# Stick-breaking attention on one core: low parts of the keys in one tile per head, doubled over the partitions, and a second score product over 128 rows instead of 64

## The chip, the core and the metric

The kernel runs on one core of one Trainium2 chip, as one launch. A core has a matrix engine (PE in the profile, TensorE in words), a vector engine (DVE, VectorE), an engine for activation functions (ACT, ScalarE), a general engine (POOL, GpSimd) and a queue that issues the transfers here (SP, SyncE). PE works in two instructions per product: a weight load (`LDWEIGHTS`, the rows PEld) of the operand that stays in the array, and the `MATMUL` that streams the other operand past it into a PSUM bank. The metric is the device time of the program in microseconds (us): 1305.93 us, the median of 3 runs before the change (1305.73 to 1306.77).

## The reference

A decoder trunk of two layers over 1024 tokens of width 1024, batch 1. Layer A is a gated short convolution. Layer B is attention with 16 heads of width 64, in which the weight of a key is a sigmoid times the product of (1 - sigmoid) over all keys between it and the query. The part that matters here, cut:

```python
def stick_breaking_attention(q, k, v):
    ...
        z = jnp.einsum('bhqd,bhkd->bhqk', qb, kb) * inv_sqrt_d
        ...
        mask = kpos < qpos
        log_beta = jax.nn.log_sigmoid(z)
        log_1m_beta = jnp.where(mask, log_beta - z, 0.0)
        suffix = lax.cumsum(log_1m_beta, axis=3, reverse=True) - log_1m_beta
        a = jnp.where(mask, jnp.exp(log_beta + suffix), 0.0)
        outs.append(jnp.einsum('bhqk,bhkd->bhqd', a.astype(vb.dtype), vb))
```

Around it stand the projections of q, k, v and a gate from the normed input, an output projection, a residual and a last norm. All of it is float32.

## The kernel before, in words

**Precision.** PE multiplies float32 data of a shortened form (`F32R`). To keep the precision, an operand x is split into a high part h (rounded to the short form) and a low part l = x - h, and a product of two operands is summed from h·h, h·l and l·h. A projection (`linear`, lines 176 to 178) is therefore three `MATMUL`s per 128 input channels, 24 per 512 tokens.

**Keys and queries.** Heads come in pairs, 8 pairs; a pair's 128 channels lie on the 128 partitions, head A (a = 0) on partitions 0 to 63 and head B (a = 1) on 64 to 127. After the projection, `keys` writes with `evacuate` (line 443 on ACT, line 444 on DVE) the high parts of both heads into one tile and the low parts into the tile `kl`. Three transfers per half of the tokens (`move`, line 440, issued by SP, 64 partitions x 512 tokens, 128 KB) then build two tiles `kh[0]`, `kh[1]`, each with the high part of one head's keys in both halves of the partitions. `queries` builds `qq[0]`, `qq[1]` likewise: the high part of one head's queries in that head's half, its low part in the other half. All these tiles are of 128 x 1024 numbers and come from the pool tag `qk`, which has 10 buffers; a pair takes five (`kl`, two `kh`, two `qq`).

**Scores.** `attention` goes, for each head a of the pair, over four groups g of two blocks of 128 queries and over chunks of up to 512 keys. Per block and chunk there are two products into one PSUM bank (tag `z`, 2 banks), with the query block of `qq` as the weights:

- line 524: all 128 rows, `qq[:, qs]` with `kh`, which gives high queries · high keys plus low queries · high keys in one pass;
- line 525: the 64 rows `own` of the head, `qq[own, qs]` with `kl[own, ...]`, which adds high queries · low keys.

A head has 12 such pairs of products: 6 that are 512 keys wide and 2 each of 384, 256 and 128; a pair of heads has 24, the program 192. Behind them follows, per block: two sigmoids on ACT (lines 530, 531), a scan on DVE (line 535), a product on POOL (line 537), transposes on PE (line 546), the split of the transposed block on ACT and DVE (lines 549, 550), and the products with the values on PE (lines 559, 560); the head's output is put together on ACT and DVE (lines 564, 565).

**Order.** The main loop runs over the pairs: attention of pair p, then the gate's projection `silu_z(p)` and the projections `project_qkv(p + 1)` of the next pair; weights are prepared by a transfer (line 144), a scaling on DVE (line 151), a split on ACT and POOL (lines 138, 139) and a sum over the shift on DVE (lines 159, 161). In the program as built the instructions of each engine stand in an order that a scheduler fixed beforehand, so that the projections of the next pair fill PE's time between the steps of the running pair's attention. Each engine works its own list from front to back and waits on semaphores of the others. SP's queue is such a list too: a transfer that waits holds up those behind it. In the last pair the place of the next projections is taken by the first part of the output projection.

Of the kernel before, what the change touches and what calls it, by code (L numbers as in the profile page):

```python
# [15 lines left out]
P = 128          # partitions  # L16
D = 1024         # model width
T = 1024         # tokens
KT = D // P      # contraction tiles
HALF = 512       # tokens per PSUM bank  # L20
NH = T // HALF
DH = 64          # head width
NPAIR = 8        # pairs of heads
EPS = 1e-6
SPILL = NPAIR - 2  # pairs whose gated output waits in DRAM
EARLY = 4        # output tiles begun before the last pair is done
WARM = (6, 6, 3)  # idle products behind the first loads
# [4 lines left out]
# columns of the packed vectors  # L32
# [4 lines left out]
def decoder_kernel(ctx, tc, vecs, xT, a_mod, kv_mod, b_mod, w_in, w_out_a, w_kv, w_qz, w_out_b, outT):  # L37
# [20 lines left out]
    # ---- constants  # L58
    vec = const.tile([P, 128], F32, name="vec")
    nc.sync.dma_start(vec, vecs)  # L60
    # zeros, then the identity: what the scan over a row of blocks adds on the diagonal
# [17 lines left out]
    # ---- [128, n * 128] -> the sums over the partitions, n columns of 128, as groups of up to 4  # L79
# [14 lines left out]
    # ---- the same as products that add up in PSUM: a sum over sources, each with its column of factors  # L94
    def column_totals(terms, n):
        ps = ps_tile("o")[:, :n]
        for k, (src, factor) in enumerate(terms):
            for i in range(n):
                # one start for the bank: the first write to each column after it replaces, the others add
                nc.tensor.matmul(ps[:, i:i + 1], lhsT=src[:, i * P:(i + 1) * P], rhs=factor,  # L100
                                 start=(k == 0 and i == 0), stop=(k == len(terms) - 1 and i == n - 1))
        return ps

    # ---- the modulation's vectors, one number per partition and column
# [15 lines left out]
    # products that nobody reads, so that TensorE's clock is up when the first ones are due  # L120
# [20 lines left out]
    # ---- weights: gain folded in, split in two parts of 12 bits, and the shift's share  # L141
# [38 lines left out]
    # ---- sums of squares by channel -> 1/rms by token, the same in every partition  # L180
# [38 lines left out]
    # ======== layer A: gated short convolution ========  # L219
# [12 lines left out]
    # the gain of one half of the channels, two row tiles of the modulation's weights at a step  # L232
# [138 lines left out]
    # ---- out-projection of layer A, residual, sums of squares  # L371
# [27 lines left out]
    # ======== layer B: stick-breaking attention ========  # L399
# [27 lines left out]
    def normalise(sl):  # L427
        # from here on these tokens have their rms in the input of layer B's projections
        for kt in range(KT):
            x = att.tile([P, HALF], F32, name="xn", tag="b", bufs=6)  # L430
            nc.sync.dma_start(x, x1_dram[kt, :, sl])
            nc.vector.tensor_mul(x, x, rbc_b[:, sl])
            split(x1h[kt][:, sl], x1l[kt][:, sl], x, nc.gpsimd)

    def project_qkv(p):
# [11 lines left out]
        # kh: the high part of one head's keys, twice; kl: the low parts of both heads' keys  # L447
        kl = qk_tile("kl")
        kh = [qk_tile("kh") for _ in range(2)]

        def keys(sl, t, bias):
            evacuate(t, bias, kh[0][:, sl], kl[:, sl])
            move(kh[1][A, sl], kh[0][B, sl])
            move(kh[1][B, sl], kh[0][B, sl])
            move(kh[0][B, sl], kh[0][A, sl])

        # qq: the high part of one head's queries, and its low part in the other half
# [11 lines left out]
        def values(src, bias):  # L469
            t = att.tile([P, HALF], F32, name="vt", tag="pt", bufs=2)  # L470
            nc.scalar.activation(t, src, AF.Identity, bias=bias)
            ps = ps_tile("tr")
            for i in range(4):
                nc.tensor.transpose(ps[:, i * P:(i + 1) * P], t[:, i * P:(i + 1) * P], ident)
            # columns: A hi, A lo, B lo, B hi
            v = att.tile([P, 4, 4, DH], F32R, name="vv", tag="vv", bufs=4)
            src = ps.rearrange("p (b a d) -> p b a d", b=4, a=2)
            nc.scalar.activation(v[:, :, 0::3, :], src, AF.Copy)
            nc.vector.tensor_tensor(v[:, :, 1:3, :], src, v[:, :, 0::3, :].bitcast(F32), op=ALU.subtract)
            vv.append(v)  # L480
# [19 lines left out]
        return [(kh[a], kl, qq[a]) for a in range(2)], vv  # L500
# [3 lines left out]
    def attention(p, heads, vv):  # L504
        o = att.tile([P, T], F32, name="o", tag="o", bufs=2)
        for a in range(2):
            kh, kl, qq = heads[a]
            own, oth = half(a), half(1 - a)
            for g in range(4):
# [5 lines left out]
                for c in reversed(range(g // 2 + 1)):  # L515
                    c0 = c * HALF
                    rows = []
                    for r in range(2):
# [6 lines left out]
                        nc.tensor.matmul(zps[:, :w], lhsT=qq[own, qs], rhs=kl[own, c0:c0 + w], start=False, stop=True)  # L525
                        b = att.tile([P, HALF], F32, name="b", tag="b", bufs=6)
                        # suffix products: a row of blocks ends in column T - 1, and column T holds zeros
# [4 lines left out]
                        # from the right: 0 above the diagonal, 1 on it, then the product of the columns passed  # L532
# [6 lines left out]
                    for jp in reversed(range(2 * c, min(2 * c + 2, g + 1))):  # L539
# [3 lines left out]
                        # blocks by (key block, query block); the last key block has one query block  # L543
# [55 lines left out]
    # ---- out-projection of layer B, residual, last norm  # L599
# [20 lines left out]
    # while the last pair's attention runs: the other pairs' share of the first tiles  # L620
# [116 lines left out]
```

## Time and profile before

| | |
|---|---|
| time, median of 3 runs | 1305.93 us (1305.73 to 1306.77) |
| profiled execution, from the first to the last instruction (span) | 1303.0 us |
| median less span (launch and end, outside the instructions) | 2.9 us |
| PE busy | 1223.5 us, 94% |
| DVE busy | 1066.1 us, 82% |
| POOL busy | 584.8 us, 45% |
| ACT busy | 507.1 us, 39% |
| transfers' share of the 16 DMA engines (main queue) | 30.3% |

The profile gives for the profiled execution the span alone, so its own whole time is taken as the span and the 2.9 us around it; a change in the span is carried over to the median of the runs. Busy times of PE are modelled: a `MATMUL` row lasts until its last result is written, while the next one starts earlier, so the time that a product takes of PE is the step from its start to the start of the next. Attention stretches from about 564 us to about 1195 us; what lies ahead is layer A and the modulation, what lies behind is the rest of the output projection and the last norm. In a row of the stretches (windows) the numbers behind an engine's name are busy us and, in brackets, instructions; PEclk is the granted clock of TensorE as a share of full speed.

### The profile page before, as it was taken

The numbers are of one execution on the slowest core, as the hardware profiler recorded it, in microseconds if no ns is written. First come the engines' busy times: TensorE is split into PE (matmuls) and PEld (weight loads), VectorE is DVE, ScalarE is ACT, GpSimd is POOL, SyncE is SP. The second block draws the span as 40 slices with busy tenths as digits, with TensorE's granted clock in tenths as the row PEclk, the third lists the DMA queues.
The fourth block names the chain that finished last, engine by engine and source line by source line (L and its number), as shares of the span: only waits on it lengthen the run. The fifth ranks groups of instructions, "written<-read, shape, count | busy, mean of one in ns | idle before, by whom it ended". The sixth has DMA issues, their size and how long they took to land.

```text
span 1303.0 us, 16390 instructions
## 1 busy us (share of the span) xinstructions
PE 1223.5 (94%) x5828; PEld 977.0 (75%) x5828; DVE 1066.1 (82%) x1575; ACT 507.1 (39%) x928; POOL 584.8 (45%) x393
## 2 busy tenths in 40 slices
PE   5899799879889999888999999999999999999995
PEld 4688588668777888766777777777777777777885
DVE  7989876888988746799889888899888898678366
ACT  3412221111211232235555555545555455556251
POOL 4623332323323354276455544646446465447334
PEclk9999899889998999888999999999999999999997
DMA  9332214243343444441212122121121212352203
GB/s 367 151 98 65 83 49 145 89 137 123 96 153 107 140 149 131 126 141 61 53 49 82 49 61 54 65 66 49 61 53 65 70 46 67 99 222 98 65 18 130
DMA packets 56450, 128.02 MB, mean 98 GB/s; under 512 B 6576, under 2 KB 10800, under 8 KB 56368
## 3 DMA queue, kind: packets, MB, share of 16 engines
q1 hardware_dynamic: 56368, 126.97, 30.3%
q8 instruction: 46, 0.75, 0.2%
q14 instruction: 36, 0.29, 0.1%
HBM read 99.68 MB, written 14.68 MB: 88 GB/s over the span
## 4 chain that ended last, share of the span: by engine, by line
PE 65%; DVE 25%; DMA 6%; issue 2%; ACT 0%; POOL 0%; SPq 0%; DVEq 0%; POOLq 0%; ACTq 0%
PE ps_mm L176 11%; PE ps_mm L177 11%; PE ps_mm L178 10%; DVE bacc L161 7%; PE ps_z L525 5%; PE ps_tr L546 5%; DVE gacc L116 4%; PE ps_o L560 3%; PE ps_o L559 3%; PE ps_z L524 3%; DMA graw<-b_mod 3%; PE ps_z L177 2%; PE ps_z L176 2%; PE ps_z L178 2%; DVE s L327 2%
## 5 line engine op out<-in xcount | busy, mean ns | idle before, releaser
L537 POOL TENSOR_TENSOR b<-b,sfx 128x128 f32<-128x128 f32 (+1 forms) x192 | 207.5, 1089 | 260.0 <-DVE sfx L535 195.8
L139 POOL TENSOR_TENSOR wlo<-raw,whi 128x1024 fp32r<-128x1024 f32 x78 | 197.5, 2534 | 281.8 <-ACT whi L138 255.4
L535 DVE TENSOR_TENSOR_SCAN sfx<-sfx,zid 128x128 f32<-128x128 f32 (+1 forms) x192 | 225.3, 1187 | 17.9 <-ACT sfx L530 17.7
L176 PE MATMUL ps_mm<-x1h,whi 128*128 128x512 f32 x480 | 195.7, 408 | 0.1
L177 PE MATMUL ps_mm<-x1l,whi 128*128 128x512 f32 x480 | 193.3, 403 | 0.0
L178 PE MATMUL ps_mm<-x1h,wlo 128*128 128x512 f32 x480 | 192.2, 400 | 0.0
L138 ACT ACTIVATE whi<-raw 128x1024 fp32r<-128x1024 f32 x78 | 82.5, 1058 | 172.0 <-issue 71.6
L530 ACT ACTIVATE sfx<-ps_z 128x128 f32<-128x128 f32 (+1 forms) x192 | 95.6, 498 | 88.4 <-PE ps_z L525 86.5
L549 ACT ACTIVATE ah<-ps_tr 128x512 fp32r<-128x512 f32 (+1 forms) x160 | 85.2, 560 | 79.2 <-PE ps_tr L546 77.1
L550 DVE TENSOR_TENSOR al<-ps_tr,ah 128x512 fp32r<-128x512 f32 (+1 forms) x160 | 96.5, 625 | 22.6 <-ACT ah L549 21.9
L161 DVE SCALAR_TENSOR_TENSOR bacc<-raw,shift_a,bacc 128x128 f32<-128x128 f32 x196 | 107.7, 561 | 2.8
L176 PEld LDWEIGHTS ps_mm<-x1h,whi 128*128 128x128 f32 x480 | 91.3, 190 | 23.7 <-issue 6.2
L177 PEld LDWEIGHTS ps_mm<-x1l,whi 128*128 128x128 f32 x480 | 91.1, 190 | 21.6 <-issue 5.4
L178 PEld LDWEIGHTS ps_mm<-x1h,wlo 128*128 128x128 f32 x480 | 91.0, 190 | 20.6 <-issue 3.3
L531 ACT ACTIVATE b<-ps_z 128x128 f32<-128x128 f32 (+1 forms) x192 | 96.1, 500 | 9.4 <-PE ps_tr L546 9.4
L116 DVE SCALAR_TENSOR_TENSOR gacc<-graw,cs,gacc 128x512 f32<-128x512 f32 x84 | 67.0, 802 | 39.0 <-DMA graw<-kv_mod 17.9
L546 PE MATMUL ps_tr<-zid,b 128*128 128x128 f32 x576 | 91.0, 275 | 1.2 <-POOL b L537 1.2
L559 PE MATMUL ps_o<-ah,vv 128*128 128x256 f32 x320 | 86.7, 288 | 0.0
L525 PE MATMUL ps_z<-kl,qq 64*128 64x128 f32 (+1 forms) x192 | 84.5, 440 | 0.0
L560 PE MATMUL ps_o<-al,vv 128*128 128x256 f32 x320 | 81.7, 294 | 0.5 <-DVE al L550 0.4
L161 DVE SCALAR_TENSOR_TENSOR bacc<-raw,shift_b,bacc 128x128 f32<-128x128 f32 x112 | 76.2, 680 | 1.3
L524 PE MATMUL ps_z<-kh,qq 128*128 128x128 f32 (+1 forms) x192 | 75.4, 393 | 0.0
(246 smaller groups left out, 2764.7 us busy)
## 6 DMA issues: line engine op xcount, KB each, us to landing
raw<-w_in SPq DMA_DIRECT2D x28, 512.0 KB, 4.2
graw<-b_mod SPq DMA_DIRECT2D x48, 256.0 KB, 2.7
stage<-a_mod SPq DMA_DIRECT2D x16, 512.0 KB, 9.6
graw<-kv_mod SPq DMA_DIRECT2D x32, 256.0 KB, 3.1
raw<-w_kv SPq DMA_DIRECT2D x16, 512.0 KB, 3.6
raw<-w_qz SPq DMA_DIRECT2D x16, 512.0 KB, 3.8
kh<-kh SPq DMA_DIRECT2D x48, 128.0 KB, 2.3
raw<-w_out_b SPq DMA_DIRECT2D x10, 512.0 KB, 3.7
```

The costliest lines, as they stand in the source:

```text
L116: nc.vector.scalar_tensor_tensor(acc[:, sl], raw, cs[:, kt:kt + 1], acc[:, sl], op0=ALU.mult, op1=ALU.add)
L139: lo_eng.tensor_tensor(lo, full, hi.bitcast(F32), op=ALU.subtract)
L161: nc.vector.scalar_tensor_tensor(acc, raw[:, kt * P:(kt + 1) * P], shift[:, kt:kt + 1], acc, op0=ALU.mult, op1=ALU.add)
L176: nc.tensor.matmul(ps, lhsT=wh, rhs=ah[kt][:, sl], start=(kt == kts[0]), stop=False)
L177: nc.tensor.matmul(ps, lhsT=wh, rhs=al[kt][:, sl], start=False, stop=False)
L178: nc.tensor.matmul(ps, lhsT=wl, rhs=ah[kt][:, sl], start=False, stop=(kt == kts[-1]))
L525: nc.tensor.matmul(zps[:, :w], lhsT=qq[own, qs], rhs=kl[own, c0:c0 + w], start=False, stop=True)
L535: nc.vector.tensor_tensor_scan(rev, rev, zid[:, z0:z0 + w][:, ::-1], sf[r][:, s0 + w:s0 + w + 1], op0=ALU.mult, op1=ALU.add)
L537: nc.gpsimd.tensor_tensor(b[:, :w], b[:, :w], sf[r][:, s0 + 1:s0 + w + 1], op=ALU.mult)
L546: nc.tensor.transpose(tp[:, s * P:(s + 1) * P], rows[r][:, jb * P - c0:(jb + 1) * P - c0], ident)
L559: nc.tensor.matmul(ops[:, cols], lhsT=vs, rhs=ah[:, rs], start=first, stop=False)
L560: nc.tensor.matmul(ops[:, cols], lhsT=vs, rhs=al[:, rs], start=False, stop=end)
```

## The change: what it does

`kl` becomes a list of two tiles. The evacuation writes the low parts of both heads into `kl[0]`, and the same three transfers that `kh` had build `kl[0]` and `kl[1]`, each with the low parts of one head's keys in both halves of the partitions. The second score product reads all 128 rows of `qq` and of the head's own `kl`; it adds high queries · low keys and also low queries · low keys. A pair takes six tiles of the tag `qk` instead of five; the tag keeps 10 buffers. Comments are removed, which moves some line numbers by one: lines 524 and 525 of before are 525 and 526 after, 474 is 475, 546 is 547.

```diff
-        # kh: the high part of one head's keys, twice; kl: the low parts of both heads' keys
-        kl = qk_tile("kl")
+
+        kl = [qk_tile("kl") for _ in range(2)]
         kh = [qk_tile("kh") for _ in range(2)]
 
         def keys(sl, t, bias):
-            evacuate(t, bias, kh[0][:, sl], kl[:, sl])
-            move(kh[1][A, sl], kh[0][B, sl])
-            move(kh[1][B, sl], kh[0][B, sl])
-            move(kh[0][B, sl], kh[0][A, sl])
+            evacuate(t, bias, kh[0][:, sl], kl[0][:, sl])
+            for k in (kh, kl):
+                move(k[1][A, sl], k[0][B, sl])
+                move(k[1][B, sl], k[0][B, sl])
+                move(k[0][B, sl], k[0][A, sl])
...
-        return [(kh[a], kl, qq[a]) for a in range(2)], vv
+        return [(kh[a], kl[a], qq[a]) for a in range(2)], vv
...
                         nc.tensor.matmul(zps[:, :w], lhsT=qq[:, qs], rhs=kh[:, c0:c0 + w], start=True, stop=False)
-                        nc.tensor.matmul(zps[:, :w], lhsT=qq[own, qs], rhs=kl[own, c0:c0 + w], start=False, stop=True)
+                        nc.tensor.matmul(zps[:, :w], lhsT=qq[:, qs], rhs=kl[:, c0:c0 + w], start=False, stop=True)
```

On SP's queue, in a middle pair, the transfers from one weight load to the next but one stand in the built program of before as:

```order
L144 DMA raw<-w_kv 128x1024
L440 DMA kh<-kh 64x512 x6
L144 DMA raw<-w_qz 128x1024
L440 DMA qq<-qq 64x512
L440 DMA qq<-ql 64x512 x2
L440 DMA qq<-qq 64x512
L440 DMA qq<-ql 64x512 x2
L144 DMA raw<-w_kv 128x1024
```

and in that of the change as:

```order
L144 DMA raw<-w_kv 128x1024
L440 DMA kh<-kh 64x512 x2
L440 DMA kl<-kl 64x512 x2
L440 DMA kh<-kh 64x512
L440 DMA kl<-kl 64x512
L440 DMA kh<-kh 64x512 x2
L440 DMA kl<-kl 64x512 x2
L440 DMA kh<-kh 64x512
L440 DMA kl<-kl 64x512
L144 DMA raw<-w_qz 128x1024
L440 DMA qq<-qq 64x512
```

Six transfers are added per pair, all ahead of the load of the query weights (`w_qz`); what follows keeps its order.

In the last pair, the load of one residual tile (line 611, the fifth of eight) also goes behind the twelve loads of the gated outputs (line 625).

On PE, DVE, ACT and POOL the lists of before and after hold the same arithmetic instructions, and apart from the first pair's attention they stand in the same order row by row. In the first pair some rows change places. On PE, around the transposes of the first pair's second half of values (`vt`), before:

```order
L176 MATMUL ps_mm<-x1h,whi 128x512
L524 MATMUL ps_z<-kh,qq 128x384
L525 MATMUL ps_z<-kl,qq 128x384
L177 MATMUL ps_mm<-x1l,whi 128x512
L178 MATMUL ps_mm<-x1h,wlo 128x512
L176 MATMUL ps_mm<-x1h,whi 128x512
L474 MATMUL ps_tr<-zid,vt 128x128 x4
L524 MATMUL ps_z<-kh,qq 128x512
L525 MATMUL ps_z<-kl,qq 128x512
```

and after:

```order
L176 MATMUL ps_mm<-x1h,whi 128x512
L475 MATMUL ps_tr<-zid,vt 128x128 x4
L177 MATMUL ps_mm<-x1l,whi 128x512
L178 MATMUL ps_mm<-x1h,wlo 128x512
L176 MATMUL ps_mm<-x1h,whi 128x512
L177 MATMUL ps_mm<-x1l,whi 128x512
L178 MATMUL ps_mm<-x1h,wlo 128x512
L525 MATMUL ps_z<-kh,qq 128x384
L526 MATMUL ps_z<-kl,qq 128x384
L525 MATMUL ps_z<-kh,qq 128x512
L526 MATMUL ps_z<-kl,qq 128x512
```

The score products of 384 and 512 keys stand a few projection products later, behind the transposes instead of around them. (The rows show the partitions of the output; the 64 rows of line 525 are its operands'.)

## The prediction

> **What bounds the kernel now.** I read the page first (span, busy shares, the chain of work that ended last), then the stretches pair by pair, then the timeline around a score product. From the page, its span, its busy times and the chain:
>
> ```profile
> span 1303.0 us, 16390 instructions
> PE 1223.5 (94%) x5828; PEld 977.0 (75%) x5828; DVE 1066.1 (82%) x1575; ACT 507.1 (39%) x928; POOL 584.8 (45%) x393
> ...
> PE ps_mm L176 11%; PE ps_mm L177 11%; PE ps_mm L178 10%; DVE bacc L161 7%; PE ps_z L525 5%; PE ps_tr L546 5%; DVE gacc L116 4%; PE ps_o L560 3%; PE ps_o L559 3%; PE ps_z L524 3%; DMA graw<-b_mod 3%; PE ps_z L177 2%; PE ps_z L176 2%; PE ps_z L178 2%; DVE s L327 2%
> ```
>
> Lines 524 and 525 stream equally many columns, yet the chain has 5% of the span for line 525 and 3% for line 524. The stretches (first pair in two parts, pairs 1 to 5, pair 6, the last pair's attention) say who sets the pace:
>
> ```profile
> 564.00:604.00 40.00, 31.26 (x116) 23.19 (x114) 39.75 (x55) 17.16 (x33) 28.11 (x19) 0.83 0.31 98
> 604.00:661.00 57.00, 57.00 (x283) 43.41 (x281) 48.70 (x69) 31.27 (x62) 31.18 (x23) 1.00 0.23 61
> 661.00:742.00 81.00, 80.98 (x408) 62.97 (x409) 72.33 (x96) 42.98 (x90) 38.96 (x33) 1.00 0.21 59
> 742.00:822.00 80.00, 80.00 (x405) 62.32 (x403) 70.48 (x96) 42.53 (x89) 38.34 (x32) 1.00 0.21 60
> 822.00:902.20 80.20, 80.20 (x405) 62.56 (x404) 71.36 (x97) 42.70 (x89) 41.95 (x33) 1.00 0.20 60
> 902.20:982.50 80.30, 80.30 (x406) 62.64 (x405) 71.17 (x97) 42.68 (x89) 41.95 (x33) 1.00 0.20 60
> 982.50:1062.80 80.30, 80.30 (x406) 62.64 (x405) 71.17 (x97) 42.69 (x89) 41.93 (x33) 1.00 0.20 60
> 1062.80:1144.50 81.70, 81.70 (x420) 64.07 (x418) 61.14 (x80) 43.13 (x90) 41.17 (x34) 1.00 0.28 88
> 1144.50:1192.50 48.00, 48.00 (x250) 36.54 (x248) 37.98 (x45) 30.46 (x66) 25.45 (x21) 1.00 0.49 176
> ```
>
> The columns are length, PE, PEld, DVE, ACT, POOL, granted clock, DMA share, GB/s. From 604 on PE is never idle, at full clock; a pair takes 80.3 us, and DVE is second with 71.2. Whether PE is busy with work is a question of the steps from one product's start to the next. The timeline:
>
> ```profile
> 811.35 0.40 PE L176 MATMUL ps_mm<-x1h,whi 128*128 128x512 f32 x1
> ...
> 811.58 0.39 PE L177 MATMUL ps_mm<-x1l,whi 128*128 128x512 f32 x1
> 811.58 0.19 PEld L178 LDWEIGHTS ps_mm<-x1h,wlo 128*128 128x128 f32 x1
> 811.81 0.39 PE L178 MATMUL ps_mm<-x1h,wlo 128*128 128x512 f32 x1
> ...
> 812.04 0.40 PE L524 MATMUL ps_z<-kh,qq 128*128 128x512 f32 x1
> ...
> 813.26 0.49 PE L524 MATMUL ps_z<-kh,qq 128*128 128x512 f32 x1
> ...
> 813.68 0.18 PEld L525 LDWEIGHTS ps_z<-kl,qq 64*128 64x128 f32 x1 [0.24 <-issue]
> 813.69 0.49 PE L525 MATMUL ps_z<-kl,qq 64*128 64x512 f32 x1
> ...
> 814.11 0.19 PEld L176 LDWEIGHTS ps_mm<-x1h,whi 128*128 128x128 f32 x1 [0.24 <-issue]
> 814.11 0.50 PE L176 MATMUL ps_mm<-x1h,whi 128*128 128x512 f32 x1
> ...
> 814.45 0.39 PE L177 MATMUL ps_mm<-x1l,whi 128*128 128x512 f32 x1
> ...
> 814.68 0.40 PE L178 MATMUL ps_mm<-x1h,wlo 128*128 128x512 f32 x1
> ```
>
> Between products of 128 rows the step is 0.23 us (811.35, 811.58, 811.81, 812.04), and the next weights load while the product before still runs (811.58). The weights of the 64-row product load only at 813.68, when nothing of line 524 is left to start, after a wait of 0.24; the weights behind it wait 0.24 again. So PE is "busy" for 80.3 us, but part of it is the array running empty twice per line 525.
>
> **The change part by part.**
>
> *The second product at 128 rows.* Lines 176 and 177 are its model: two 128-row products with the same weights, 0.23 apart. For 512 keys the steps now are 0.43 (813.26 to 813.69), 0.42 (to 814.11) and 0.34 (to 814.45), together 1.19 where three plain ones take 0.69: 0.50 lost. The narrower ones, from the last pair (384 keys, then 128):
>
> ```profile
> 1178.50 0.30 PE L524 MATMUL ps_z<-kh,qq 128*128 128x128 f32 x1
> 1178.73 0.32 PE L525 MATMUL ps_z<-kl,qq 64*128 64x128 f32 x1
> 1178.99 0.73 PE L176 MATMUL ps_mm<-oh,whi 128*128 128x512 f32 x2
> ...
> 1182.59 0.34 PE L524 MATMUL ps_z<-kh,qq 128*128 128x384 f32 x1
> 1182.86 0.43 PE L525 MATMUL ps_z<-kl,qq 64*128 64x384 f32 x1
> 1183.23 0.39 PE L560 MATMUL ps_o<-al,vv 128*128 128x256 f32 x1
> 1183.45 0.23 PE L559 MATMUL ps_o<-ah,vv 128*128 128x128 f32 x1
> ```
>
> At 384 keys the steps are 0.27, 0.37 and 0.22 (0.86), against 0.17, 0.17 and 0.12 by the 0.23 per 512 columns (0.46): 0.40 lost. At 128 they are 0.23 and 0.26 against, as an estimate, 0.11 each (half of a 512-column step; less is not assumed, since each product loads weights too): 0.27, and 0.1 for the product behind, as at the other widths: 0.37. With 12 of a pair's 24 at 512 and 12 narrower at about 0.41, the mean is 0.455, 10.9 us per pair of heads, 87 us for the 192. PE's own need falls from 80.3 to 69.4 us per pair.
>
> The Trainium skill, "TensorE: Matmul & The Clock Gate", Part 3 (What overlaps and what doesn't), speaks against this: a weight load overlaps a running product only where the row group differs. By it two 128-row products could not overlap either, and the sum would be 0 instead of 87; the load at 811.58 under the running line 177 says otherwise. The skill's "TensorEngine Tiling (Array Packing)", Key Properties, has the rule that fits the row: changing the tiling mode drains the array, so that 87 would be the sum.
>
> *Who is late next.* DVE needs 71.2 us per pair and PE then 69.4: DVE, which holds back the products of lines 559 and 560 by its split (line 550). What DVE waited for in one period (860.28 to 940.56), by the waits:
>
> ```profile
> DVE o L565 <- ACT o L564: 5.5, 2, 3.4
> ...
> DVE sfx L535 <- ACT sfx L530: 2.5, 2, 1.3
> ...
> DVE bias L169 <- PE ps_mm L168: 1.0, 2, 0.5
> ```
>
> All 9.0 us come from PE directly or through ACT, so an earlier PE should shrink them, not to nothing: the steps from PE over ACT stay. The bounds: DVE as the bound was busy 39.75 of 40 us in the stretch from 564 (0.99), and today it reaches 71.2 of 80.3 (0.89). I take 0.96, some 3 us idle per pair, nearer to 0.99, because most of the 9.0 us lies in a few long waits (5.5 us in two, the longest 3.4) that a late PE makes. DVE's work itself need not stay equal:
>
> ```profile
> 807.38 1.82 DVE L161 SCALAR_TENSOR_TENSOR bacc<-raw,shift_b,bacc 128x128 f32<-128x128 f32 x1
> ...
> 810.92 0.32 DVE L161 SCALAR_TENSOR_TENSOR bacc<-raw,shift_b,bacc 128x128 f32<-128x128 f32 x1
> ```
>
> The same operation takes 0.32 or 1.82 us, which I read as DVE being held up by POOL; POOL's 42 us per pair get denser in a shorter pair. That is in the 0.96.
>
> *The sum by stretches.*
> - 564 to 604: DVE is busy 39.75 of 40; nothing gained. The moved rows of the first pair lie here: two to four microseconds either way, taken as 0.
> - 604 to 661: at a full pair's rate of loss (10.9 of 80.3) PE needs 49.3, DVE 48.7. With both equal I take 52: 5 us (2 to 7.5).
> - Pairs 1 to 5: 401.8 us long, DVE busy 356.5 in all. At 0.96 that is 371: 30 us. At 0.99, 360: 42. At 0.91, 392: 10.
> - Pair 6: DVE needs only 61.1, PE 70.8: PE stays the bound, 10 us (8 to 11).
> - The last pair: PE 48.0 less some 10, DVE 38.0, again equal: 5 us (2 to 9).
>
> Together 50 us (22 to 69). The span goes from 1303.0 to 1253; with the 2.9 us that lie between the span and the median of the runs, 1256.
>
> *The added transfers.* Three more per half of the tokens, 48 in all. The issues on SP in a middle pair and the landing time of the model, the moves of `kh`, by the transfers:
>
> ```profile
> kh<-kh SPq DMA_DIRECT2D x48, 128.0 KB, 2.3
> ```
>
> ```profile
> 935.03 14.13 SPq L440 DMA_DIRECT2D kh<-kh  x6
> 953.87 0.34 SPq L144 DMA_DIRECT2D raw<-w_qz  x1
> 954.26 0.46 SPq L440 DMA_DIRECT2D qq<-qq  x1
> ```
>
> The six end at 949.16 and the next row, the load of `w_qz`, issues at 953.87: 4.7 us of slack. A half adds three issues of 0.46 and little waiting, since the landing (2.3) is waited for together with that of `kh`: 1.4 to 3.7 us, and the first half's are done before the second half's keys are there. So the load stays where it is or slips by a microsecond, and its weights are needed tens of microseconds later: 0. Without that cover it would be up to 3.7 us per pair, 26 in all. On PE, DVE and ACT nothing is added.
>
> *The sixth tile.* Two pairs would want 12 of 10 buffers, so the next pair's `qq` must take buffers of the running pair. By the built program's addresses they take those of head A's `kh` and `qq` each time, free when head B begins; the queries are written in the middle of head B (954.26). 0.
>
> **The rivals.**
>
> 1. *PE and DVE take turns.* The fixed order makes each wait for the other's last result, and only a third of the 50 survives: DVE at 0.91 and the lower ends above, 22 us or less: 1284 (1275 to 1297). For it: two engines at 69.4 and 71.2 that hand each block to and fro. Against: a pair's 192 projection products (eight halves of 24), which need nothing of the blocks, stand between them.
> 2. *DVE is no bound*, because its long operations shrink as often as they grow: PE's whole 87 less the first part's: 1224 (to 1237). Against: nothing takes work off DVE.
> 3. *The change does not do what it says*: the second load still waits (the row-group rule), or what makes it wait is the bank that it adds to and not the row count. 1306. Against: 811.58, where a product of 128 rows adds to the bank of the one before without a wait.
> 4. *Slower: the clock.* When PE waits for DVE the granted clock drops, as in the stretch from 564, where PE was busy 31.26 of 40 and the clock 0.83. At 0.83 a pair of 69.4 us of PE work takes 83.6, 3.3 more than now, and the six pairs lose 20 us: 1326. It decides from a clock of 69.4 / 80.3 = 0.86 downwards. Against: in that stretch PE was idle 8.7 us of 40, in the forecast it is under 5 of 74, in small pieces. The skill's "TensorE: Matmul & The Clock Gate" (Why this matters for your kernels) names idle gaps of over about 3 us as the trigger; by that the clock stays at 1.00.
> 5. *The tile or the queue after all*: the queries wait for head B's end, two landings of 2.3 us in a row, 4.6 us per pair and 32 in all off the 50: 1288. Against: the addresses and the 4.7 us of slack.
>
> **How the numbers follow.** The forecast, 1240 to 1272 around 1256, has 0.62; rival 1 has 0.18, rival 2 0.08, rivals 3, 4 and 5 0.04 each. To hold 8 in 10 the range takes in half of rival 2 and most of rival 1: 1232 to 1290. A measurement of this kernel tells about 0.2% from no change; faster by more than that are the forecast and rivals 1, 2 and 5: 0.92; same is rival 3: 0.04; slower is rival 4: 0.04.
>
> **What would show it right or wrong.** Right: no wait for issue before the second product's weights, steps of 0.23 from the first to the second and to the next; a pair of 72 to 76 us; DVE at 0.94 to 0.99 of it; PE no longer at 100% in pairs 1 to 5, waiting for DVE's split or POOL's product, and still at 100% in pair 6. Wrong: steps still of 0.42 (rival 3), PE at 100% with pairs of 70 us (rival 2), a clock below 1.00 behind 620 us (rival 4), SP's loads waiting on the key moves (rival 5).

## The result, and the profile after

The change makes the kernel faster: 1267.89 us, the median of 4 runs (1264.91 to 1275.82), against 1306.11 us for the kernel before, beside it on the same chip (4 runs, 1305.73 to 1306.77). The ratio, taken over all the runs, is 0.9716, with an interval of 0.9685 to 0.9746. The forecast was 1256 us, with 1232 to 1290 around it: a gain of 50 us was expected, 38 came.

The page of the changed kernel, its span, its busy times and its chain of waits:

```profile
span 1274.0 us, 16465 instructions
...
PE 1165.9 (92%) x5828; PEld 976.5 (77%) x5828; DVE 1076.9 (85%) x1575; ACT 500.1 (39%) x928; POOL 588.9 (46%) x393
...
PE 48%; DVE 36%; DMA 7%; issue 5%; ACT 2%; POOL 1%; SPq 0%; DVEq 0%; ACTq 0%; POOLq 0%
DVE bacc L161 10%; PE ps_mm L178 7%; PE ps_mm L177 7%; PE ps_mm L176 7%; DVE sfx L536 5%; DVE gacc L116 4%; PE ps_tr L547 3%; DMA graw<-kv_mod 3%; PE ps_o L561 3%; PE ps_z L176 2%; PE ps_z L177 2%; PE ps_z L178 2%; PE ps_tr L176 2%; PE ps_tr L177 2%; PE ps_tr L178 2%
```

PE lost 58 us of busy time with equally many instructions. The two score products, 8% of the chain before, are no longer among its first lines, and at its head stands DVE's line 161, the sum over the shift.

This profiled execution is the slowest of its four runs, 1275.82 us. The changed kernel therefore ran again without an edit, `again` below, and the readings of places are taken from that trace (span 1260.9), which is of the fastest of its own four runs. Its timeline around two blocks of queries in the middle of the program, PE and then one of the weight loads:

```profile
892.00 0.42 PE L525 MATMUL ps_z<-kh,qq 128*128 128x384 f32 x1
892.26 0.34 PE L526 MATMUL ps_z<-kl,qq 128*128 128x384 f32 x1
892.44 0.40 PE L525 MATMUL ps_z<-kh,qq 128*128 128x512 f32 x1
892.67 0.40 PE L526 MATMUL ps_z<-kl,qq 128*128 128x512 f32 x1
892.90 0.39 PE L178 MATMUL ps_mm<-x1h,wlo 128*128 128x512 f32 x1
```

```profile
892.44 0.19 PEld L526 LDWEIGHTS ps_z<-kl,qq 128*128 128x128 f32 x1
```

From the first product of 512 keys to the second, and from there to the next, the step is now 0.23 us (892.44, 892.67, 892.90). The weights of line 526 load at 892.44, at the start of the product before, instead of behind it. How much waiting there was in the whole program, the view of one line says; the kernel before, line 525:

```profile
L525 PEld LDWEIGHTS ps_z<-kl,qq x192: 182/183/286, 564.1 to 1198.7; 64*128 64x128 f32 x192
...
  issue: 37.4, 152
```

Ahead of 152 of the 192 loads the load engine waited for issue, 37.4 us in all. The same view for line 526 of the changed kernel lists no wait at all.

The stretches of `again`, cut at the first score product of each pair (the pairs 1 to 6, then the last pair's attention; columns as before: length, PE, PEld, DVE, ACT, POOL, clock, DMA share, GB/s):

```profile
656.50:733.50 77.00, 73.74 (x412) 62.68 (x410) 71.93 (x95) 42.33 (x91) 38.35 (x32) 1.00 0.25 69
733.50:809.00 75.50, 72.13 (x400) 61.41 (x399) 72.73 (x97) 42.08 (x88) 42.16 (x33) 1.00 0.27 76
809.00:883.50 74.50, 72.23 (x405) 62.01 (x404) 72.07 (x97) 41.67 (x89) 43.92 (x33) 1.00 0.26 75
883.50:958.00 74.50, 72.24 (x405) 62.00 (x404) 72.04 (x97) 41.66 (x89) 43.61 (x33) 1.00 0.26 75
958.00:1032.60 74.60, 72.36 (x406) 62.03 (x406) 72.11 (x97) 41.91 (x90) 42.73 (x33) 1.00 0.27 76
1032.60:1107.00 74.40, 73.38 (x419) 63.66 (x418) 63.09 (x81) 42.15 (x89) 43.02 (x35) 1.00 0.34 100
1107.00:1153.00 46.00, 42.98 (x255) 36.71 (x254) 40.12 (x48) 31.17 (x69) 29.81 (x22) 1.00 0.53 195
```

A middle pair takes 74.5 us instead of 80.3. PE is busy 72.2 of them and DVE 72.1: two engines at 0.97, where before one was at 1.00 and the other at 0.89. The clock stays at 1.00. What each still waits for, over the six pairs (656.5 to 1107.0):

```profile
PE ps_o L561 <- DVE al L551: 14.4, 16, 1.4
```

```profile
DVE o L566 <- ACT o L565: 9.8, 10, 3.5
DVE al L551 <- ACT ah L550: 8.0, 4, 3.1
DVE sfx L536 <- ACT sfx L531: 5.4, 7, 1.6
```

PE waits 14.4 us, all of it for DVE's split; DVE waits 23.2 us, all of it for ACT, which stands between PE and DVE: ACT's own longest waits in this stretch are for products of PE (53.3, 46.4 and 40.0 us).

### The profile page after: what moved, and what is told of

Its sections match the earlier page's. It is cut to its first block, busy times and chain, and to the rows that moved or that the text cites. A ratio compares the mean times of both kernels' runs of the same rounds, so it can differ in the third digit from the quotient of the medians.

```text
span 1274.0 us, 16465 instructions
## 1 busy us (share of the span) xinstructions
PE 1165.9 (92%) x5828; PEld 976.5 (77%) x5828; DVE 1076.9 (85%) x1575; ACT 500.1 (39%) x928; POOL 588.9 (46%) x393
## 4 chain that ended last, share of the span: by engine, by line
PE 48%; DVE 36%; DMA 7%; issue 5%; ACT 2%; POOL 1%; SPq 0%; DVEq 0%; ACTq 0%; POOLq 0%
DVE bacc L161 10%; PE ps_mm L178 7%; PE ps_mm L177 7%; PE ps_mm L176 7%; DVE sfx L536 5%; DVE gacc L116 4%; PE ps_tr L547 3%; DMA graw<-kv_mod 3%; PE ps_o L561 3%; PE ps_z L176 2%; PE ps_z L177 2%; PE ps_z L178 2%; PE ps_tr L176 2%; PE ps_tr L177 2%; PE ps_tr L178 2%
## 5 line engine op out<-in xcount | busy, mean ns | idle before, releaser
L538 POOL TENSOR_TENSOR b<-b,sfx 128x128 f32<-128x128 f32 (+1 forms) x192 | 212.1, 1114 | 220.7 <-DVE sfx L536 162.4
L176 PE MATMUL ps_mm<-x1h,whi 128*128 128x512 f32 x480 | 191.5, 399 | 3.5 <-ACT x1h L138 1.8
L177 PE MATMUL ps_mm<-x1l,whi 128*128 128x512 f32 x480 | 190.0, 396 | 0.5 <-POOL x1l L139 0.5
L561 PE MATMUL ps_o<-al,vv 128*128 128x256 f32 x320 | 82.8, 297 | 16.7 <-DVE al L551 16.5
L161 DVE SCALAR_TENSOR_TENSOR bacc<-raw,shift_b,bacc 128x128 f32<-128x128 f32 x112 | 81.4, 727 | 1.2
L561 PEld LDWEIGHTS ps_o<-al,vv 128*128 128x128 f32 x320 | 60.6, 190 | 27.3 <-DVE al L551 24.2
L161 DVE SCALAR_TENSOR_TENSOR bacc<-raw,shift_kv,bacc 128x128 f32<-128x128 f32 x112 | 74.7, 667 | 2.3
```

What stands on the lines that cost most here:

```text
L161: nc.vector.scalar_tensor_tensor(acc, raw[:, kt * P:(kt + 1) * P], shift[:, kt:kt + 1], acc, op0=ALU.mult, op1=ALU.add)
L176: nc.tensor.matmul(ps, lhsT=wh, rhs=ah[kt][:, sl], start=(kt == kts[0]), stop=False)
L177: nc.tensor.matmul(ps, lhsT=wh, rhs=al[kt][:, sl], start=False, stop=False)
L538: nc.gpsimd.tensor_tensor(b[:, :w], b[:, :w], sf[r][:, s0 + 1:s0 + w + 1], op=ALU.mult)
L561: nc.tensor.matmul(ops[:, cols], lhsT=vs, rhs=al[:, rs], start=False, stop=end)
```

## The experiments

The theory under test has two halves: the second product was dear because its 64 rows stood between products of 128, and behind that DVE sets the pace. Its rivals: a product of 64 rows is dear by itself, or the moves and the order make the difference; and behind that the two engines take turns, so that a lighter DVE would bring little.

### The change once more

`again`: the changed kernel, no edit.

> The changed kernel once more, unchanged. In its first profile the attention stage gained 42 us, but the first pair's start lost 5 us and the code ahead of it, which is the same in both kernels, came 8 us late. If that delay is chance (DVE and POOL holding each other up at other moments), the runs scatter between 1262 and 1276 and this profile has another delay ahead of 535 us; if it belongs to the built program, the runs stay at 1268 plus or minus 2 with the same 8 us. Either way a middle pair takes 74.5 us.

1266.19 us (4 runs, 1262.76 to 1267.94) against 1306.95 (13 runs, 1304.72 to 1313.14): 0.968 (0.965 to 0.9711). From here on the gain is counted in this trace, span 1260.9 against 1303.0: 42.1 us. It is of the fastest of the changed kernel's eight runs, so it shows more than the medians do, 38.2 us above and 40.8 here.

The trace shown first lies 13.4 us behind it at the first score product (579.75 against 566.33), though the instructions ahead of it are the same. By the starts of the same instructions it was some 8 us late at 535 us already, in layer A, and it lost the rest in the next stretch, here in the first profile and in `again`:

```profile
535.00:580.00 45.00, 34.93 (x150) 27.92 (x148) 37.82 (x71) 10.69 (x16) 19.94 (x12) 0.90 0.46 136
```

```profile
535.00:580.00 45.00, 40.02 (x181) 32.61 (x180) 41.75 (x78) 13.73 (x21) 23.93 (x15) 0.98 0.51 155
```

Fewer instructions of every engine fall into it, and the clock is lower. Since `again` lacks the delay, the expectation's second reading, that the delay belongs to the built program, falls. Single operations of DVE take much longer in one of the traces than in the other (one of line 116, which starts at 441.82, 2.83 us, and in `again` 0.74), but how such differences add up to 13 us was not settled. The changed kernel's eight runs scatter over 13 us (1262.76 to 1275.82).

### The moves without the wider product

`moves_only`: the change, with the second product back at 64 rows.

```diff
-nc.tensor.matmul(zps[:, :w], lhsT=qq[:, qs], rhs=kl[:, c0:c0 + w], start=False, stop=True)
+nc.tensor.matmul(zps[:, :w], lhsT=qq[own, qs], rhs=kl[own, c0:c0 + w], start=False, stop=True)
```

> The changed kernel with its two tiles of low parts and its 48 added transfers, but the second product at 64 rows again (the result is the same as before). Theory: the gain lies in the product's rows alone and the transfers cost only what the first pair's start lost: 1306 to 1316, a middle pair 80.3 us. Rival: transfers and the sixth tile cost in every pair, hidden in the gain: above 1320.

1309.59 us (10 runs, 1306.79 to 1315.82): 1.0027 (1.0007 to 1.0046), as the first of the two expectations had it. A middle pair is as it was:

```profile
824.00:904.20 80.20, 80.20 (x405) 62.59 (x404) 71.36 (x97) 42.58 (x88) 41.96 (x33) 1.00 0.24 69
```

The two tiles, the 48 transfers and the moved rows bring nothing; they cost 2.6 us of the median, with an interval from 0.9 to 6. Which of the three costs it was not separated.

### The wider product without the moves

`rows_only`: the kernel before, with all 128 rows read from its one `kl`. Left out is the building of the doubled tiles, so the second product multiplies the low queries with the other head's low keys; the shapes and the amount of work on PE are those of the change.

```diff
-nc.tensor.matmul(zps[:, :w], lhsT=qq[own, qs], rhs=kl[own, c0:c0 + w], start=False, stop=True)
+nc.tensor.matmul(zps[:, :w], lhsT=qq[:, qs], rhs=kl[:, c0:c0 + w], start=False, stop=True)
```

> The kernel before with the second product over all 128 rows of the one tile of low parts, without the added transfers and the sixth tile (the sum then contains a product of the wrong parts; the doubling of the low parts is what is left out). Theory: a middle pair takes 74.5 us as in the changed kernel, and the first pair starts as before: 1258 to 1264. If the start's 5 us do not come from the transfers, it stays at 1264 to 1270. If the transfers cost in every pair, the pair falls to 71 us: below 1250.

1266.04 us (4 runs, 1262.94 to 1266.98): 0.9678 (0.965 to 0.9707), the same as `again`, and as the second of the three expectations had it. A middle pair:

```profile
809.80:884.30 74.50, 72.24 (x405) 62.01 (x404) 72.02 (x97) 41.68 (x89) 43.92 (x33) 1.00 0.22 64
```

Length and busy times are those of `again` to 0.1 us. The row count alone makes the gain, and the transfers that the change needs for it are hidden.

### What a change of the row count costs

`probe`: the changed kernel with a list of products that nobody uses behind the last norm, each with its own weight load, all into one bank (`full_r` is all 128 rows, `lo_r` the first 64). 60 more of 128 rows ahead of the list, not shown in the cut, keep PE at work until it begins.

```diff
...
+    def of(r, n=HALF, first=False, last=False):
+        return dict(out=ps[:, :n], lhsT=oh[0][r, :P], rhs=ol[0][r, :n], start=first, stop=last)
...
+    for _ in range(24): nc.tensor.matmul(**of(full_r))
+    for _ in range(12):
+        nc.tensor.matmul(**of(full_r))
+        nc.tensor.matmul(**of(lo_r))
+    for _ in range(24): nc.tensor.matmul(**of(lo_r))
+    for _ in range(6):
+        nc.tensor.matmul(**of(full_r))
+        nc.tensor.matmul(**of(full_r))
+        nc.tensor.matmul(**of(lo_r))
+        nc.tensor.matmul(**of(lo_r))
+    for _ in range(24): nc.tensor.matmul(**of(full_r, P))
+    for _ in range(12):
+        nc.tensor.matmul(**of(full_r, P))
+        nc.tensor.matmul(**of(lo_r, P))
...
```

> The changed kernel with rows of products behind its last norm, into one PSUM bank that nobody reads, to measure steps by themselves: 24 of 128 rows, 24 in turn of 128 and 64 rows, 24 of 64 rows, 24 in twos (128, 128, 64, 64), all 512 columns wide, then 24 of 128 rows and 24 in turn at 128 columns. If the change of the row count empties the array, steps are 0.23, 0.42, 0.23 and the mean of both (0.33). If each 64-row product does it by itself, the third row has 0.42 too; if what counts is that weights are loaded for the same rows (the row-group rule), the first row has 0.42. At 128 columns: 0.11 and 0.25.

One run, 1314.81 us with the added products (what counts is their steps). Its timeline; a row "x24" stands for 24 products in a row, and lines 707 and 709 are of 128 rows, 710 and 712 of 64, 714 and 715 of 128, 716 of 64, 719 and 721 of 128 rows with 128 columns, 722 of 64 rows with 128 columns:

```profile
1271.53 5.60 PE L707 MATMUL ps_z<-ol,oh 128*128 128x512 f32 x24
1276.97 0.39 PE L709 MATMUL ps_z<-ol,oh 128*128 128x512 f32 x1
1277.29 0.50 PE L710 MATMUL ps_z<-ol,oh 64*128 64x512 f32 x1
1277.72 0.49 PE L709 MATMUL ps_z<-ol,oh 128*128 128x512 f32 x1
1278.14 0.50 PE L710 MATMUL ps_z<-ol,oh 64*128 64x512 f32 x1
...
1287.01 5.64 PE L712 MATMUL ps_z<-ol,oh 64*128 64x512 f32 x24
1292.59 0.50 PE L714 MATMUL ps_z<-ol,oh 128*128 128x512 f32 x1
1292.93 0.40 PE L715 MATMUL ps_z<-ol,oh 128*128 128x512 f32 x1
1293.25 0.50 PE L716 MATMUL ps_z<-ol,oh 64*128 64x512 f32 x1
...
1300.53 2.90 PE L719 MATMUL ps_z<-ol,oh 128*128 128x128 f32 x24
1303.26 0.28 PE L721 MATMUL ps_z<-ol,oh 128*128 128x128 f32 x1
...
1303.72 0.33 PE L721 MATMUL ps_z<-ol,oh 128*128 128x128 f32 x1
1303.98 0.32 PE L722 MATMUL ps_z<-ol,oh 64*128 64x128 f32 x1
1304.23 0.33 PE L721 MATMUL ps_z<-ol,oh 128*128 128x128 f32 x1
```

- 24 products of 128 rows in a row: (1276.97 - 1271.53) / 24 = 0.227 us each.
- 24 products of 64 rows in a row: (1292.59 - 1287.01) / 24 = 0.23 us each. By itself a product of 64 rows is not dear: that rival falls.
- Alternating: 0.43 and 0.42 (1277.29, 1277.72, 1278.14): 0.20 more per change, in either direction.
- Two and two: 0.34 and 0.32 (1292.59, 1292.93, 1293.25), so one change per two products, its 0.20 spread over the step across it and the step behind it.
- With 128 columns: 0.114 in a row, 0.26 and 0.25 when alternating: 0.14 per change. This holds for the first ten products of the alternating row; from about 1306 us on the granted clock is 0.50 and the steps are 0.40.

All steps are those of the expectation's first reading, a change of the row count.

The Trainium skill, "TensorEngine Tiling (Array Packing)", Key Properties, says that changing the tiling mode drains the array. The steps agree, though they show lost time and not the drain itself, and only these runs give the price: 0.2 us at 512 columns. The rule weighed against the change in the prediction, that a weight load overlaps only where the row group differs ("TensorE: Matmul & The Clock Gate", Part 3, What overlaps and what doesn't), fails on the 0.227: all 24 products there have the same rows, and each loads its weights while the one before runs.

### DVE made lighter, after and before

`less_dve`: the change, with seven of the eight terms of the sum over the shift (line 161) left out in layer B, about 13 us of DVE per pair (72.0 less 59.0 in the rows; the expectation had 18). `less_dve_old`: the same left out of the kernel before.

```diff
-    def shift_terms(raw, shift):
+    def shift_terms(raw, shift, n=KT):
...
-        for kt in range(1, KT):
+        for kt in range(1, n):
...
-        return (hi, lo), shift_bias(shift_terms(raw, shift), "mm")
+        return (hi, lo), shift_bias(shift_terms(raw, shift, 1), "mm")
```

> The changed kernel with seven of the eight terms of the shift's sum (line 161) left out in layer B, so that DVE has some 18 us less to do per pair and is far from being the bound; the result lacks these terms. Theory A (the prediction's sum): PE itself needs 69.4 us per pair, so the pair falls from 74.5 to about 70 and pair 6 from 74.5 to 71; 1235 to 1245 in all. Theory B: the cost of a 64-row product was put too high, PE itself needs 72 us per pair and shares the bound with DVE: the pair falls only to 72 to 73, pair 6 stays within a microsecond of 74; 1248 to 1256.

> The same seven terms left out of the kernel before, as the control: if PE with its 64-row products was the only bound there, a middle pair stays at 80.3 us within 0.5 and only the first pair's start gains: 1298 to 1306. If DVE had a share in it, the pair falls below 79.5.

`less_dve`: 1237.23 us (4 runs, 1232.69 to 1241.5), 0.9466 (0.9431 to 0.9502) of the kernel before and 29 us under `again`. `less_dve_old`: 1303.0 us (10 runs, 1301.21 to 1305.41), 0.9966 (0.9954 to 0.9977), 3.5 us under the kernel before. The same work taken off DVE is worth 29 us with the change and 3.5 without it: DVE's time lay hidden behind PE's before, and is a bound now. A middle pair of `less_dve`, then of `less_dve_old`:

```profile
869.00:940.40 71.40, 71.40 (x406) 61.98 (x405) 58.95 (x68) 42.11 (x89) 42.54 (x32) 1.00 0.29 78
```

```profile
898.90:979.20 80.30, 80.30 (x405) 62.57 (x404) 57.62 (x68) 43.43 (x89) 41.96 (x32) 1.00 0.21 60
```

In both PE is never idle, so these rows measure PE's own need: 80.3 us per pair before and at most 71.4 after (short waits can hide in PE's modelled rows). That lies between the pairs of theory A (about 70) and theory B (72 to 73); the time lies in A's range. The 64 rows cost 80.3 - 71.4 = 8.9 us per pair, 0.37 us for each of 24 products, 71 us for the 192. In the prediction that was 0.455 and 87.

### DVE's scaling on POOL, and on ACT

Is DVE's list a bound that a real version can move? `gain_on_pool` gives the scaling of the weights of layer B (line 151, four of 128 x 1024 per pair, (14.1 + 12.1) / 5 = 5.2 us of DVE per pair in `again`) to POOL:

```diff
...
-            nc.vector.tensor_tensor(
+            eng.tensor_tensor(
...
-        raw, hi, lo = load_weights(src, gain, *place)
+        raw, hi, lo = load_weights(src, gain, *place, eng=nc.gpsimd)
```

> The changed kernel with the gain's multiplication of layer B's weights (line 151, 5.3 us of DVE per pair) on POOL; the result is the same. If DVE's list alone is what holds PE up, a pair falls to 72 to 73 us and the kernel to 1252 to 1258. If POOL's products for the attention are what is late then (POOL gets some 10 us more per pair, and DVE and POOL hold each other up), the pair stays at 74 to 76: 1262 to 1275.

`gain_on_act` gives it to ACT, in eight pieces of 128 columns, each with its own gain:

```diff
...
+            if by_act:
+                for kt in range(KT):
+                    k = slice(kt * P, (kt + 1) * P)
+                    nc.scalar.activation(w[:, k], raw[:, k], AF.Copy, scale=gain[:, kt:kt + 1])
...
-        raw, hi, lo = load_weights(src, gain, *place)
+        raw, hi, lo = load_weights(src, gain, *place, by_act=not place)
```

> The changed kernel with that multiplication on ACT instead, as eight pieces per weight (apart from the first pair's first value weights); the result is the same. ACT has 42 of 74.5 us busy and does not hold up DVE in the trace. A pair at 72 to 73 us and 1250 to 1258 if DVE's list is what holds PE up; 74 to 77 and 1262 to 1280 if ACT's longer list delays the sigmoids.

On POOL: 1291.51 us (4 runs, 1288.03 to 1295.16), 0.9886 (0.9854 to 0.9918), so 25 us slower than `again`. On ACT: 1249.31 us (4 runs, 1247.84 to 1250.43), 0.9559 (0.954 to 0.9577), 17 us faster than `again`. The time on POOL is above both of its expected ranges, the one on ACT just below the first of its own. The same 5.2 us off DVE, and 42 us between the two results. The line where they went, DVE's sum over the shift in the pairs 1 to 5 of `again`, then of `gain_on_pool` (busy us, mean ns of one), with what `gain_on_pool` adds on POOL:

```profile
L161 DVE SCALAR_TENSOR_TENSOR bacc<-raw,shift_b,bacc 128x128 f32<-128x128 f32 x70 | 55.9, 799 | 0.7
...
L151 DVE TENSOR_TENSOR raw<-raw,gain_b 128x1024 f32<-128x1024 f32 x10 | 14.1, 1407 | 0.0
...
L151 DVE TENSOR_TENSOR raw<-raw,gain_kv 128x1024 f32<-128x1024 f32 x10 | 12.1, 1209 | 0.0
```

```profile
L161 DVE SCALAR_TENSOR_TENSOR bacc<-raw,shift_b,bacc 128x128 f32<-128x128 f32 x70 | 65.1, 930 | 1.3
```

```profile
L151 POOL TENSOR_TENSOR raw<-raw,gain_b 128x1024 f32<-128x1024 f32 x10 | 20.2, 2022 | 0.2
```

On POOL the scaling takes 2.0 us instead of 1.2 to 1.4, and the same 70 operations of DVE get 0.13 us longer each. Most of what came off DVE's list comes back as longer operations: over the pairs 1 to 5 DVE is busy 360.9 us in `again`, 356.4 in `gain_on_pool` and 334.6 in `gain_on_act`, where some 26 us were taken off. These pairs take 387.1 us in `gain_on_pool` against 376.1; another 12 us of the 27 between the two spans lie ahead of them (668.8 against 656.5). The longest middle pair of `gain_on_pool`, and PE's waits for DVE's split over the whole program:

```profile
899.40:981.90 82.50, 75.97 (x406) 64.63 (x405) 74.32 (x94) 43.18 (x91) 48.44 (x38) 0.96 0.24 69
```

```profile
PE ps_o L561 <- DVE al L551: 30.1, 26, 2.6
```

DVE is busy 74.3 us in this pair, though 5.2 us lighter by its list, PE waits 30.1 us for the split instead of 16.5 in the first profile of the change, and the clock falls to 0.96. That DVE and POOL hold each other up can be seen at one place in `again`: DVE, then POOL, at the same moment:

```profile
848.81 3.52 DVE L161 SCALAR_TENSOR_TENSOR bacc<-raw,shift_kv,bacc 128x128 f32<-128x128 f32 x2
```

```profile
848.03 3.05 POOL L139 TENSOR_TENSOR wlo<-raw,whi 128x1024 fp32r<-128x1024 f32 x1 [1.24 <-ACT whi L138]
851.04 1.14 POOL L538 TENSOR_TENSOR b<-b,sfx 128x512 f32<-128x512 f32 x1
```

Two of line 161 take 3.52 us here, the shortest of them anywhere 0.32. The first ends at 851.23, 0.15 us behind POOL's split, the second at 852.33, 0.15 us behind POOL's next operation. That is the rule and not one place: of the 139 operations of line 161 in the pairs 1 to 5 of `again`, 61 start while POOL is at work, and every one of these ends 0.15 us behind POOL's operation (mean 1.32 us); the 78 others take 0.34 on average and none over 0.36. It holds the other way too: POOL's split takes 2.44 to 2.46 us where 0.2 us of an operation of line 161 are left at its start, and 3.03 to 3.05 where 0.85 of a scan are left. The Trainium skill, "SBUF — State Buffer", SBUF: two separate sides, tells of one port pair that DVE (with two inputs from SBUF) and GpSimd take from each other as a lock, for a whole instruction; these rows and ends agree with it.

On ACT the scaling makes no operation of DVE longer to speak of (the 26 us come off whole). ACT was busy 41.7 us of 74.5, and the eight pieces raise that to 49.5 to 53.1. The expectation's remark that ACT does not hold up DVE doesn't fit the 23.2 us above, but ACT's own longest waits there are for PE. The boundaries of the pairs shift in `gain_on_act` (its pairs 1 to 5 have 392 to 419 products), so its pairs are compared as a sum: they take 370.1 us against 376.1 in `again`, and the first pair 81.3 against 90.1.

### Both on ACT

`act_both`: as `gain_on_act`, and the first term of the shift (line 159) of layer B on ACT too. `act_again`: `gain_on_act` beside it, for the same chip.

```diff
...
-        nc.vector.tensor_scalar(acc, raw[:, 0:P], shift[:, 0:1], None, op0=ALU.mult)
+        if by_act:
+            nc.scalar.activation(acc, raw[:, 0:P], AF.Copy, scale=shift[:, 0:1])
+        else:
+            nc.vector.tensor_scalar(acc, raw[:, 0:P], shift[:, 0:1], None, op0=ALU.mult)
...
```

> The kernel with the gain on ACT, and besides the first of the eight terms of the shift's sum in layer B (line 159 of before, 2.6 us of DVE per pair) on ACT; the result is the same. If DVE's share is what still keeps pairs at 72 to 76 us in that kernel, they come to 71.4 to 73, PE's own need, and the time is 1240 to 1247. If the uneven pairs (71.7 and 76 in turn) come from ACT's longer list, it is 1249 to 1256.

> The kernel with the gain on ACT alone once more, on the same chip, for the comparison: 1247 to 1251.

`act_both`: 1239.63 us (4 runs, 1239.2 to 1240.36), 0.9488 (0.9472 to 0.9505). `act_again`: 1248.88 us (4 runs, 1245.88 to 1251.27), 0.9556 (0.9529 to 0.9582), the same as `gain_on_act`. So DVE's share was what kept the pairs long, as the first of the two expectations had it; the time is 0.4 us below its range. A middle pair of `act_both`:

```profile
939.30:1011.70 72.40, 71.67 (x406) 62.03 (x405) 64.87 (x89) 52.80 (x126) 41.36 (x33) 1.00 0.27 77
```

PE is back at 0.99 of the pair, which is 1 us above PE's own need of 71.4, and DVE at 0.90. By the medians this version lies 26.6 us under the changed kernel (`again`), 66 us under the kernel before (1305.7 to 1307.0 beside all these runs), and within 2.4 us of `less_dve`, which leaves work out.

## Why the prediction was right, and where its sizes were off

**The mechanism** holds in its main steps: the loss sits at the change of row count (`rows_only` has all of the gain, `moves_only` none), the steps fell to 0.23, the wait for issue is gone, DVE comes up beside PE, the clock stays. One sign failed: PE was to stay at 100% in pair 6, and is at 0.99 there (73.38 of 74.40). The time lies in the forecast's own range, 1240 to 1272.

**The sum by stretches**, with the gains up to the first score product of each pair in `again`:

| stretch | forecast | measured |
|---|---|---|
| up to the end of the first pair (660.9 before, 656.5 after) | 5 | 4.4 |
| pairs 1 to 5 (401.8 before, 376.1 after) | 30 | 25.7 |
| pair 6 (81.7 before, 74.5 after) | 10 | 7.3 |
| from the last pair to the end (158.5 before, 153.9 after) | 5 | 4.6 |
| together | 50 | 42 |

By the medians, 38 to 41 us, the forecast is some 10 us too high. The 2.9 us between span and time, too, hold more than launch and end: for the profiled execution of `again` the difference is 1.9 (1262.76 less 1260.9).

*Start and first pair.* The first score product comes 2.3 us later (566.3 against 564.0), within the two to four that the moved rows were given, and the first pair, 6.8 us shorter, gives it back. `rows_only`, without the moved rows, begins at 564.6 and reaches the second pair at 656.5 too, so the moved rows are worth nothing by then.

*Pairs 1 to 5.* DVE's share was put at 0.96, and it is 360.9 / 376.1 = 0.96. The term that was mis-sized is DVE's work: 356.5 us were carried over, but the five rows add up to 360.9. Those 4.4 us, over 0.96, are 4.6 of the 5 by which 376.1 lies above the forecast's 371. The prediction had seen that DVE's operations stretch when POOL gets denser, and had meant the 0.96 to cover it; it needed a term of its own. By the prediction's own reckoning, with DVE's old work, the share is 356.5 / 376.1 = 0.95. The added work is line 161's: the 70 operations shown above with 55.9 us in `again` took 50.4 in the pairs 1 to 5 of before. Of all 139 of the line, 45 started while POOL was at work before, and 61 do after. The line grew by 12.0 us, and shorter operations elsewhere, of line 159 above all (4.9), give a part back. That the share itself came to 0.96 is in part luck, since it was chosen with DVE as the only bound, and two engines bind here.

*PE's own need.* The step "0.455 us per product, PE's need falls to 69.4" is off: 0.37 and 71.4, by `less_dve`. The three steps at 813.26 were added up to 0.50 for one 64-row product, but the row ahead of them is another 64-row product:

```profile
812.84 0.50 PE L525 MATMUL ps_z<-kl,qq 64*128 64x512 f32 x1
```

By the probe a change spreads its 0.20 over the step across it and the step behind it. The step from 813.26 also holds the second half of the change made there, which belongs to the product at 812.84: the three steps held two changes and half of a third. Two changes are 0.40 at 512 columns, and 0.29 at 128 (twice 0.14). With 12 of the 24 at 512 and, as an estimate, the widths between on the line from 0.29 to 0.40, a pair comes to 8.7 us, against 8.9 measured. That the step was mis-sized did little harm in the pairs 1 to 5, where DVE's 72 us stood in the way, and shows in *pair 6*: PE needs 81.7 - 8.9 = 72.8 there, not 70.8; it was busy 73.4 of 74.4 and waited 1.0 us for DVE's split. Of the 2.7 us by which the gain fell short, 2 are this.

**"DVE is the bound"** was too simple. With PE at 71.4 and DVE at 72.1 the two are equal, and the pair lies 2.4 us above the longer: PE waits 14.4 us for DVE's split and DVE 23.2 us for PE's results by way of ACT. Rival 1 had this mechanism and the wrong price, 0.91 and 1284. Rival 2, without DVE as a bound, was put at 1224 (to 1237); `less_dve` is that case on the chip, at 1237, with 71 us of PE's work gone and not 87.

**The zeros.** The transfers: `rows_only` without them is as fast as `again` with them. In `again` SP's list at a pair's keys and queries:

```profile
927.52 1.10 SPq L440 DMA_DIRECT2D kl<-kl  x2
...
930.42 0.46 SPq L440 DMA_DIRECT2D kl<-kl  x1
932.68 0.34 SPq L144 DMA_DIRECT2D raw<-w_qz  x1
933.11 0.47 SPq L440 DMA_DIRECT2D qq<-qq  x1
```

Behind the last move of `kl`, which is over at 930.88, there are 1.8 us until the load of `w_qz`; 4.7 were free before, and 4.7 are in `rows_only`, whose pairs are as short and whose moves are the old ones (928.79 to 933.49). So the added moves take 2.9 us of the slack, within the 1.4 to 3.7 estimated, and don't use it up. The sixth tile: the queries' moves follow `w_qz` within 0.5 us, as before; rival 5 falls. Only in `moves_only`, where PE is the bound, do the transfers, the tile and the moved rows together show 2.6 us. Rival 3 falls by `rows_only`. Rival 4, the clock, does not come with the change (1.00 in all six pairs), but its mechanism exists: `gain_on_pool`, where PE waits longer, falls to 0.96 in one pair, with no wait of PE over 2.6 us in it.

## What to carry to other kernels

A product that uses fewer rows than its neighbours costs two changes of the row count, and rows that do nothing useful can be cheaper than the change; products of one row count in a row would by the probe's steps save it too, which no run of the kernel tried. Before an engine's saving is priced, its own need and that of the second engine should be read per stage: here 71 us came off PE's work and 42 off the time, because the second engine stood 9 us per pair behind the first. Relief for the second engine has to go to one that doesn't hold it up: the same 5.2 us per pair were worth +25 us on POOL and -17 us on ACT.

## What the runs showed of the hardware that was not expected

- A change between products of 64 and of 128 rows costs 0.20 us at 512 columns and 0.14 at 128, in either direction; among their own kind products of 64 rows step at 0.23 us, as those of 128 do.
- Work moved from DVE to POOL came back on DVE: the mean of line 161 rose from 0.80 to 0.93 us while DVE's list was 5.2 us shorter per pair.
- An operation of line 161 that starts while POOL is at work ends 0.15 us behind POOL's operation (61 of 61 in `again`, pairs 1 to 5); of the 78 that start while POOL is idle none takes over 0.36 us.
- The granted clock fell to 0.96 over a pair of 82.5 us in which PE was busy 76.0, and stayed at 1.00 over pairs of 74.5 with 72.2. In the probe it was 0.50 from 1306.5 to 1311.3 us, where products of 128 columns alternate between 128 and 64 rows and PE's rows leave no gap.
- One execution of the changed kernel came 13 us later to the first score product than another, with the same instructions ahead of it; the cause is open.
